# Hybrid decoder trunk on one core: order of the attention opening (dense keys and queries of head 0, value tiles, rotated queries of heads 2 and 3, key latents' sums)

## The chip, the cores and the metric

The kernel runs on one core of one Trainium2 chip. The metric is the device time of one execution in microseconds. Three runs of the kernel before gave 2683.34, 2685.63 and 2686.16 us; their median is 2685.63 us.

## What is computed

Two layers act on x of 1024 tokens by 1024 columns in float32. The part that matters here is one of the three mixers, the attention of each layer (MLA):

```
h = rms_norm(x);  p = h @ w_in                      # 1024 x 2640
c_q (384), c_kv (256), k_pe (64) = first 704 columns of p
q  = rms_norm(c_q) @ w_uq      # 4 heads x (128 plain + 64 rotary)
kv = rms_norm(c_kv) @ w_ukv    # 4 heads x (128 key + 128 value)
q_pe, k_pe -> rotated with cos and sin (k_pe is shared by the heads)
s = (q_nope @ k_nope^T + q_pe @ k_pe^T) / sqrt(192), causal
o = softmax(s) @ v             # then rms_norm over 512 columns
```

Beside it stand a gated linear attention and an RWKV-7 recurrence with a state per head. The three outputs go through w_out, and a gated feed-forward part with a convolution of width 3 ends the layer. A last rms_norm gives the output.

## The kernel before, in words

Everything is laid out with features on the 128 partitions and the 1024 tokens along the free dimension. A float32 product is made of three matmuls in the fast format: each operand is split into a rounded high part and a low rest, and `mm3` (line 97 issues every such matmul) sums high x high, high x low and low x high. A projection tile of 128 features over 8 blocks of 128 inputs is so 2 halves x 8 x 3 = 48 matmuls of 512 columns. The last five projection tiles of a layer (lines 738 to 753) are two of key latents (`ckv`) and three of query latents (`cq`). They alternate between two PSUM buffers ("big"), and each half is read from PSUM by ScalarE (line 744, high part), VectorE (line 745, low part) and ScalarE again (line 748 or 751, square). The squares are summed over the tiles into one buffer `acc` (tag T1, one buffer, so the query latents' `acc` takes the place of the key latents'). `stats` then sums `acc` over the partitions with eight one-column matmuls (line 731; the profile counts 16 records, as float32 goes in two passes) and makes the scale `rkv` (keys) or `rq` (queries) of each token.

Background work (generators in a list) is woven in by `spend`: each group of matmuls adds its nominal time, and for each 2.4 us of it (`Q_IN`; 0.9 in the attention) `tick` takes one step of every generator. `delay(n, gen)` lets n ticks go by first. At this place VectorE also runs a long elimination (lines 699 to 706) for the recurrence.

The opening of the attention (lines 1018 to 1100) then goes, in program order: load and split weights for the rotated queries of heads 0 and 1 (`wq_pe(0)`); load cos, sin and the key's rotary rows (`kraw`, and `krot` with its halves exchanged); `dense_w(0)`, the weights of head 0's plain keys and queries, through one staging buffer; `q_pe`, 18 matmuls for two heads' rotary queries, evacuated into `raw` (line 1055), four copies on ScalarE's queue that write `rot` with halves exchanged (line 1058), and `rope` (lines 1043 to 1045: POOL rot x sin, VectorE raw x cos, VectorE the sum); the split into `QP` (lines 1073, 1074) for heads 0 and 1; the key's rotation and its split `khh`, `kll` (lines 1076 to 1078); value tiles 0 to 3; a second `q_pe` for heads 2 and 3, split (lines 1085, 1086) and stored to `qdr` in DRAM by four stores on SyncE's queue (lines 1089, 1090), to be read back when head 2 comes; `Rk`, the token scales spread over the partitions (lines 1091 to 1095: transposes, ScalarE copies); value tiles 4 to 7; three ticks of the recurrence (`rwkv_chunks`, which takes its buffers from the weight pool, so it needs those of both `q_pe` back); and last `dense_k(0)` and `dense_q(0)`, 12 and 18 matmuls with their evacuations (lines 1111 to 1113 and 1123, 1124). A value tile is six matmuls into one of two PSUM banks "a" and a ScalarE copy (line 1039). `raw`, `rot` and the transposed attention weights `pT` (lines 1155, 1157) share the tag PT with two buffers.

Then for each head and block of queries: `scores` (line 97, softmax in lines 1137 to 1143), `trans` (line 1153: transposes of the weights, copied into `pT`), and `pv` (line 1164).

The order on each engine is fixed when the program is built. A planner takes the instructions in program order as priority, lets a later one go ahead where its own estimates say that an earlier one is not ready, and assigns buffers; at run time each engine goes through its list in order. So program order is a preference, and the trace shows for instance the second `q_pe` ahead of most value tiles. The second layer runs the same code.

Of the kernel before, what the change touches and what calls it, by code (L numbers as in the profile page):

```python
# [21 lines left out]
NT = T // 128  # L22
# [39 lines left out]
def trunk(ctx: ExitStack, tc: tile.TileContext, A, out, offs):  # L62
# [27 lines left out]
    def delay(n, gen):  # L90
        for _ in range(n):
            yield
        yield from gen
# [36 lines left out]
    def aps():  # L130
        return psp.tile([128, 512], F32, tag="a", name="psa")
# [172 lines left out]
    for l in range(DEPTH):  # L304
# [423 lines left out]
        def stats(acc, rs, width):  # L728
            sps = aps()
            for i in range(NT):  # L730
                pe.matmul(sps[:, i:i + 1], lhsT=acc[:, i * 128:(i + 1) * 128], rhs=ones, start=True, stop=True)
            act.activation(rs, sps[:, 0:NT], AF.Copy)
            rstd(rs, rs, NT, 1.0 / width, EPS)
            if rs is rq:
                pool.tensor_scalar(rq, rq, 192 ** -0.5, 1.0, ALU.mult, ALU.mult)
            yield

        for dst, K, gname, rs, width in ((ckv, 2, "mla_kv_norm_g", rkv, 256), (cq, 3, "mla_q_norm_g", rq, 384)):
            acc = tt(1, "acc")
            for k in range(K):  # L740
                ps = in_tile()
                g = col(gname, k)
                for n in range(2):
                    act.activation(dst[0][k][:, HALF[n]], ps[n], AF.Copy, scale=g)
                    dve.scalar_tensor_tensor(dst[1][k][:, HALF[n]], ps[n], g, dst[0][k][:, HALF[n]].bitcast(F32),
                                             ALU.mult, ALU.subtract)
                    if k == 0:
                        act.activation(acc[:, HALF[n]], ps[n], AF.Square)  # L748
                    else:
                        sq = rtp.tile([128, 512], F32, tag="csq", name="csq")  # L750
                        act.activation(sq, ps[n], AF.Square)
                        pool.tensor_tensor(acc[:, HALF[n]], acc[:, HALF[n]], sq, ALU.add)
            bg.append(delay(2, stats(acc, rs, width)))
        drain()
        tmps.close()
        right.close()
# [254 lines left out]
        def wq_pe(h):  # L1011
            return split_w(wp, 3, 128, [(64 * j, WQ[:, 192 * (h + j) + 128:192 * (h + j) + 192]) for j in range(2)])
# [4 lines left out]

        vwh, vwl = wq.pop(0)[0]
        w_pe = [wq_pe(0)]
        cos = pg("P", "cos", bufs=2)  # L1020
        sin = pg("P", "sin", bufs=2)
        nc.sync.dma_start(out=cos, in_=A["rope"][0])
        nc.sync.dma_start(out=sin, in_=A["rope"][1])
        kraw = pg("kn0", "kraw")
        krot = pg("kn1", "krot")
        for b in range(2):
            nc.sync.dma_start(out=kraw[64 * b:64 * b + 64, :], in_=kdr)
            nc.sync.dma_start(out=krot[64 * b:64 * b + 32, :], in_=kdr[32:64, :])
            nc.sync.dma_start(out=krot[64 * b + 32:64 * b + 64, :], in_=kdr[0:32, :])
        wts = dense_w(0, dve)  # L1030

        v = ap.tile([128, NT, 512], F32, name="v")

# [5 lines left out]
            act.activation(v[:, i, :], ps, AF.Copy, scale=rkv[:, i:i + 1])  # L1039
            spend(1.28)  # L1040

        def rope(raw, rot):
            pool.tensor_tensor(rot, rot, sin, ALU.mult)
            dve.tensor_tensor(raw, raw, cos, ALU.mult)
            dve.tensor_tensor(raw, raw, rot, ALU.add)

        def q_pe(w):
            ps = bigps()
            mtile(ps, 128, 3, w, cq)
            ps = halves(ps)  # L1050
            raw = pg("PT", "qraw", F32R, bufs=2)
            rot = pg("PT", "qrot", F32R, bufs=2)
            fr, ft = raw.bitcast(F32), rot.bitcast(F32)
            for n in range(2):
                act.activation(fr[:, HALF[n]], ps[n], AF.Copy)
            for b in range(4):
                o = 32 * (b ^ 1)
                nc.scalar.dma_start(out=ft[32 * b:32 * b + 32, :], in_=fr[o:o + 32, :])
            rope(fr, ft)
            return raw, rot  # L1060

        khh = pg("khh", "khh", F32R)
        kll = pg("kll", "kll", F32R)
        Rk = pg("Rk", "Rk")

        raw, _ = q_pe(w_pe.pop())
        w_pe.append(wq_pe(2))
        raw = raw.bitcast(F32)
        QP = []
        for j in range(2):  # L1070
            rows, orow = slice(64 * j, 64 * j + 64), slice(64 - 64 * j, 128 - 64 * j)
# [1 line left out]
            act.activation(q[rows, :], raw[rows, :], AF.Copy)  # L1073
            dve.tensor_tensor(q[orow, :], raw[rows, :], q[rows, :].bitcast(F32), ALU.subtract)
            QP.append(q)
        rope(kraw, krot)
        act.activation(khh, kraw, AF.Copy)
        dve.tensor_tensor(kll, kraw, khh.bitcast(F32), ALU.subtract)
        rb = pg("qn1", "rb")
        dve.tensor_copy(rb.rearrange("p (i d) -> p i d", i=NT),  # L1080
                        rkv.rearrange("p (i o) -> p i o", o=1).to_broadcast([128, NT, 128]))
        for i in range(4):
            v_tile(i)
        raw, rot = q_pe(w_pe.pop())
        act.activation(rot, raw.bitcast(F32), AF.Copy)
        dve.tensor_tensor(raw, raw.bitcast(F32), rot.bitcast(F32), ALU.subtract)
        for j in range(2):
            rows, orow = slice(64 * j, 64 * j + 64), slice(64 - 64 * j, 128 - 64 * j)
            nc.sync.dma_start(out=qdr[j][rows, :], in_=rot[rows, :].bitcast(F32))
            nc.sync.dma_start(out=qdr[j][orow, :], in_=raw[rows, :].bitcast(F32))  # L1090
        for b in range(2):
            ps = aps()
            for i in range(4):
                pe.transpose(ps[:, i * 128:(i + 1) * 128], rb[:, (4 * b + i) * 128:(4 * b + i + 1) * 128], ident)
            act.activation(Rk[:, b * 512:(b + 1) * 512], ps, AF.Copy)
        for i in range(4, 8):
            v_tile(i)
        bg.append(rwkv_chunks())
        for _ in range(3):
            tick()  # L1100

        heads = {}

# [120 lines left out]
                yield  # L1224

        heads[0] = (dense_k(0, wts[0]), dense_q(0, wts[1]), QP[0])
        t1 = t2 = None

        def flush(n):
# [9 lines left out]
        for h in range(4):  # L1239
            for at, i in enumerate((3, 4, 0, 5, 1, 6, 2, 7) if h == 0 else range(NT)):  # L1240
                if h == 3 and i == 0:
                    bg.append(early_wout())
                r = scores(h, i)
                if h < 3 and at == 3:
                    wts = dense_w(h + 1)
                if at == NT - 1 and h < 3:
                    kn = dense_k(h + 1, wts[0])
                    flush(1)
                    t1 = (h, i, *r)
                    qn = dense_q(h + 1, wts[1])  # L1250
                    if h == 0:
                        heads[1] = (kn, qn, QP[1])
                        Q2 = [None, None]
                        Q2[0] = pg("QP0", "QPr", F32R)
                        nc.sync.dma_start(out=Q2[0].bitcast(F32), in_=qdr[0])
                    elif h == 1:
                        heads[2] = (kn, qn, Q2[0])
                        Q2[1] = pg("QP1", "QPr", F32R)
                        nc.sync.dma_start(out=Q2[1].bitcast(F32), in_=qdr[1])
                    else:  # L1260
                        heads[3] = (kn, qn, Q2[1])
                else:
                    flush(1)
                    t1 = (h, i, *r)
# [521 lines left out]
```

## Time and profile before

| | |
|---|---|
| median of three runs | 2685.63 us |
| the profiled execution | 2680.95 us |
| its span | 2679.2 us |
| VectorE busy | 1686.9 us, 63% |
| ScalarE busy | 1154.1 us, 43% |
| POOL busy | 1049.1 us, 39% |
| mean granted TensorE clock | 0.983 of full |

The opening comes twice: in layer 0 the last projection matmul starts at 324.57 us and the first scores at 367.54 us. TensorE's busy time counts a matmul from start to its modelled end, so a stretch at half clock is busy too; the granted clock (PEclk) must be read beside it. In a timeline the bracket holds the idle time of the engine just before the instruction and what released it.

### The profile page before, as it was taken

The numbers are of one execution on the slowest core, as the hardware profiler recorded it, in microseconds if no ns is written. First come the engines' busy times: TensorE is split into PE (matmuls) and PEld (weight loads), VectorE is DVE, ScalarE is ACT, GpSimd is POOL, SyncE is SP. The second block draws the span as 40 slices with busy tenths as digits, with TensorE's granted clock in tenths as the row PEclk, the third lists the DMA queues.
The fourth block names the chain that finished last, engine by engine and source line by source line (L and its number), as shares of the span: only waits on it lengthen the run. The fifth ranks groups of instructions, "written<-read, shape, count | busy, mean of one in ns | idle before, by whom it ended". The sixth has DMA issues, their size and how long they took to land. (4 is left out here: it accounts for less than half of the span.)

```text
span 2679.2 us, 36147 instructions
## 1 busy us (share of the span) xinstructions
PE 2582.8 (96%) x13842; PEld 2093.7 (78%) x13842; DVE 1686.9 (63%) x2390; ACT 1154.1 (43%) x1894; POOL 1049.1 (39%) x903
## 2 busy tenths in 40 slices
PE   8999989999899999999999999999998999999997
PEld 7668778888778888777776787788886888887786
DVE  3446665655976666776733565656469756668775
ACT  4221255554544544543352222546444445455333
POOL 4446432132554444231234563323326544452311
PEclk9999999999999999999999999999999999999999
DMA  4102221133232222685411122212342222217941
GB/s 131 32 24 56 67 72 43 51 117 119 78 103 71 94 72 70 206 206 124 116 38 32 32 71 67 62 32 68 119 133 64 90 84 78 88 56 236 216 114 63
DMA packets 246333, 240.93 MB, mean 90 GB/s; under 512 B 40376, under 2 KB 188304, under 8 KB 246160
## 3 DMA queue, kind: packets, MB, share of 16 engines
q1 hardware_dynamic: 210816, 203.31, 24.1%
q0 software_dynamic: 14336, 27.27, 5.8%
q10 hardware_dynamic: 21008, 8.04, 1.2%
q8 instruction: 109, 1.79, 0.3%
q14 instruction: 64, 0.52, 0.1%
HBM read 178.80 MB, written 53.48 MB: 87 GB/s over the span
## 5 line engine op out<-in xcount | busy, mean ns | idle before, releaser
L97 PE MATMUL psb<-hl,wh 128*128 128x512 f32 (+2 forms) x704 | 269.8, 384 | 1.5 <-DVE hl L208 1.5
L97 PE MATMUL psb<-hh,wh 128*128 128x512 f32 (+2 forms) x704 | 266.4, 380 | 4.2 <-ACT acc L748 3.3
L97 PE MATMUL psb<-hh,wl 128*128 128x512 f32 (+2 forms) x704 | 268.7, 382 | 0.7 <-POOL wl L258 0.7
L97 PE MATMUL psr<-B,RG 128*128 128x512 f32 x1032 | 253.9, 391 | 0.7 <-DVE RG L1299 0.7
L97 PE MATMUL psa<-T,RG 128*128 128x512 f32 x1008 | 246.6, 390 | 1.0 <-ACT RG L1298 1.0
L1299 POOL TENSOR_TENSOR RG<-S_m,RG 128x512 fp32r<-128x512 f32 x86 | 121.5, 1412 | 274.2 <-ACT RG L1298 239.1
L97 PEld LDWEIGHTS psr<-B,RG 128*128 128x128 f32 x1032 | 193.5, 188 | 43.8 <-DVE RG L1299 1.6
L97 PEld LDWEIGHTS psa<-T,RG 128*128 128x128 f32 x1008 | 189.1, 188 | 42.5 <-ACT RG L1298 1.8
L1298 ACT ACTIVATE RG<-S_m 128x512 fp32r<-128x512 f32 x176 | 111.0, 630 | 226.3 <-PE psa L97 118.2
L97 PEld LDWEIGHTS psb<-hh,wl 128*128 128x128 f32 (+1 forms) x704 | 132.5, 188 | 33.4 <-issue 10.5
L97 PEld LDWEIGHTS psb<-hh,wh 128*128 128x128 f32 (+1 forms) x704 | 132.1, 188 | 33.5 <-issue 4.9
L97 PEld LDWEIGHTS psb<-hl,wh 128*128 128x128 f32 (+1 forms) x704 | 132.6, 188 | 29.5 <-issue 5.4
L97 PE MATMUL psr<-T,RG 128*128 128x512 f32 x528 | 136.4, 400 | 11.0 <-ACT T L1298 9.2
L97 PEld LDWEIGHTS psr<-T,RG 128*128 128x128 f32 x528 | 101.4, 192 | 35.5 <-ACT T L1298 10.1
L258 POOL TENSOR_TENSOR wl<-ws,wh 128x1024 fp32r<-128x1024 f32 (+1 forms) x40 | 91.4, 2287 | 92.3 <-ACT wh L256 61.4
L1496 DVE SCALAR_TENSOR_TENSOR psb<-uv,convc,psb 128x1023 f32<-128x1023 f32 x72 | 92.6, 1286 | 55.2 <-ACT psb L1494 54.2
L1298 ACT ACTIVATE de<-R 128x1024 fp32r<-128x1024 f32 x67 | 69.2, 1052 | 117.7 <-PE psb L97 35.5
L1606 POOL DMA_DIRECT2D R<-fdr x48 | 43.9, 945 | 187.6 <-issue 50.4
L97 PE MATMUL psb<-de 128*128 128x512 f32 x384 | 108.9, 402 | 6.6 <-DVE acc_kb L1677 6.6
L254 POOL TENSOR_TENSOR ws<-ws,pcol 128x1024 f32<-128x1024 f32 x36 | 76.5, 2127 | 87.2 <-DMA ws<-in_w_in 77.9
L256 ACT ACTIVATE wh<-ws 128x1024 fp32r<-128x1024 f32 (+2 forms) x44 | 43.7, 994 | 154.9 <-PE psb L97 146.1
L1299 DVE TENSOR_TENSOR de<-R,de 128x1024 fp32r<-128x1024 f32 x67 | 84.2, 1268 | 40.2 <-ACT de L1298 40.2
(552 smaller groups left out, 6590.5 us busy)
## 6 DMA issues: line engine op xcount, KB each, us to landing
wu_m<-in_ffn_w_up SPq DMA_DIRECT2D x88, 512.0 KB
fdr<-acc SPq DMA_DIRECT2D x44, 512.0 KB
R<-fdr SPq DMA_DIRECT2D x88, 256.0 KB
R<-in_ffn_w_down SPq DMA_DIRECT2D x88, 256.0 KB
ws<-in_w_in SPq DMA_DIRECT2D x38, 512.0 KB
R<-fdr POOLq DMA_DIRECT2D x48, 256.0 KB, 5.5
y_m<-ydr SPq DMA_DIRECT2D x16, 512.0 KB
xmid<-x SPq DMA_DIRECT2D x16, 512.0 KB
```

What stands on the lines that cost most here:

```text
L97: pe.matmul(o, lhsT=l, rhs=r, start=first, stop=last, skip_group_check=on)
L254: eng.tensor_tensor(ws, ws, g.rearrange("p (k o) -> p k o", o=1).to_broadcast([128, K, M]), ALU.mult)
L256: act.activation(wh, ws, AF.Copy)
L258: eng.tensor_tensor(wl, ws, wh.bitcast(F32), ALU.subtract)
L1298: act.activation(d[0], s, AF.Copy)
L1299: eng.tensor_tensor(d[1], s, d[0].bitcast(F32), ALU.subtract)
L1496: dve.scalar_tensor_tensor(a[:, d:T], u[:, 0:T - d], conv[:, 2 - d, jj:jj + 1], a[:, d:T], ALU.mult, ALU.add)
L1606: pool.dma_start(out=o, in_=x, accum_op=ALU.add)
```

## The change

Five things are moved, and nothing is computed differently.

1. `stats` of both latents waits six ticks in place of two.
2. The weights of head 0's dense keys and queries are loaded and split right behind `wq_pe(0)`, ahead of the loads of cos, sin and the key's rotary rows. `kraw` and `krot` take the buffers qn0 and qn1 (those of head 0's dense queries) in place of kn0 and kn1, and `rb`, from which `Rk` is made, takes kn1.
3. `rope` becomes `turn`, which makes the two products and leaves the sum to the caller. `Rk` is made right after the first `q_pe`, then come the key's two products, then the sum and split of the queries of heads 0 and 1, then the key's sum and split.
4. `dense_k(0)` and `dense_q(0)` come ahead of all value tiles; value tiles 0 to 3, the second `q_pe` (products only), value tiles 4 to 7 and the three ticks follow.
5. The sum and split of the queries of heads 2 and 3 and their four stores (`keep_q2`) come behind the first block's scores.

```diff
-            bg.append(delay(2, stats(acc, rs, width)))
+            bg.append(delay(6, stats(acc, rs, width)))
...
         w_pe = [wq_pe(0)]
+        wts = dense_w(0, dve)
         cos = pg("P", "cos", bufs=2)
...
-        kraw = pg("kn0", "kraw")
-        krot = pg("kn1", "krot")
+        kraw = pg("qn0", "kraw")
+        krot = pg("qn1", "krot")
...
-        wts = dense_w(0, dve)
...
-        def rope(raw, rot):
+        def turn(raw, rot):
             pool.tensor_tensor(rot, rot, sin, ALU.mult)
             dve.tensor_tensor(raw, raw, cos, ALU.mult)
-            dve.tensor_tensor(raw, raw, rot, ALU.add)
...
-            rope(fr, ft)
+            turn(fr, ft)
             return raw, rot
...
-        raw, _ = q_pe(w_pe.pop())
+        rb = pg("kn1", "rb")
+        dve.tensor_copy(rb.rearrange("p (i d) -> p i d", i=NT),
+                        rkv.rearrange("p (i o) -> p i o", o=1).to_broadcast([128, NT, 128]))
+        raw, rot = q_pe(w_pe.pop())
         w_pe.append(wq_pe(2))
+        for b in range(2):
+            ps = aps()
+            for i in range(4):
+                pe.transpose(ps[:, i * 128:(i + 1) * 128], rb[:, (4 * b + i) * 128:(4 * b + i + 1) * 128], ident)
+            act.activation(Rk[:, b * 512:(b + 1) * 512], ps, AF.Copy)
+        turn(kraw, krot)
         raw = raw.bitcast(F32)
+        dve.tensor_tensor(raw, raw, rot.bitcast(F32), ALU.add)
         QP = []
...
-        rope(kraw, krot)
+        dve.tensor_tensor(kraw, kraw, krot, ALU.add)
         act.activation(khh, kraw, AF.Copy)
         dve.tensor_tensor(kll, kraw, khh.bitcast(F32), ALU.subtract)
-        rb = pg("qn1", "rb")
...
-        for i in range(4):
-            v_tile(i)
-        raw, rot = q_pe(w_pe.pop())
-        act.activation(rot, raw.bitcast(F32), AF.Copy)
-        dve.tensor_tensor(raw, raw.bitcast(F32), rot.bitcast(F32), ALU.subtract)
...
         heads[0] = (dense_k(0, wts[0]), dense_q(0, wts[1]), QP[0])
+        for i in range(4):
+            v_tile(i)
+        raw2, rot2 = q_pe(w_pe.pop())
+        for i in range(4, 8):
+            v_tile(i)
+        bg.append(rwkv_chunks())
+        for _ in range(3):
+            tick()
+
+        def keep_q2():
+            dve.tensor_tensor(raw2.bitcast(F32), raw2.bitcast(F32), rot2.bitcast(F32), ALU.add)
+            act.activation(rot2, raw2.bitcast(F32), AF.Copy)
+            dve.tensor_tensor(raw2, raw2.bitcast(F32), rot2.bitcast(F32), ALU.subtract)
+            for j in range(2):
+                rows, orow = slice(64 * j, 64 * j + 64), slice(64 - 64 * j, 128 - 64 * j)
+                nc.sync.dma_start(out=qdr[j][rows, :], in_=rot2[rows, :].bitcast(F32))
+                nc.sync.dma_start(out=qdr[j][orow, :], in_=raw2[rows, :].bitcast(F32))
...
                 r = scores(h, i)
+                if h == 0 and at == 0:
+                    keep_q2()
```

## Rows read from the trace of the kernel before

**Rows 1.** The page, part 1: busy us, share of the span, instructions, by engine.
```profile
PE 2582.8 (96%) x13842; PEld 2093.7 (78%) x13842; DVE 1686.9 (63%) x2390; ACT 1154.1 (43%) x1894; POOL 1049.1 (39%) x903
```

**Rows 2.** Waits of TensorE, whole span: who waited for whom, us in total, times, longest.
```profile
PE psa L731 <- POOL acc L752: 5.8, 4, 2.5
PE psb L97 <- DVE kn L1113: 5.2, 2, 3.9
...
PE psr L840 <- DMA rcb<-zdr: 3.5, 2, 2.5
PE psb L97 <- ACT acc L748: 3.3, 1, 3.3
```

**Rows 3.** Timeline, ScalarE, layer 0: start us, us, instruction, [idle before, releaser].
```profile
282.96 1.06 ACT L256 ACTIVATE wh<-ws 128x1024 fp32r<-128x1024 f32 x1 [0.81 <-PE psb L97]
...
295.54 0.60 ACT L751 ACTIVATE csq<-psb 128x512 f32<-128x512 f32 x1 [1.93 <-DVE ckv_m L745]
...
301.82 1.06 ACT L256 ACTIVATE wh<-ws 128x1024 fp32r<-128x1024 f32 x1 [2.17 <-PE psb L97]
...
313.89 1.06 ACT L321 ACTIVATE vwh<-vws 128x1024 fp32r<-128x1024 f32 x1 [6.97 <-PE psb L97]
...
324.77 0.52 ACT L256 ACTIVATE wh<-ws 128x384 fp32r<-128x384 f32 x1 [5.15 <-PE psb L97]
```

**Rows 4.** Timeline, TensorE, layer 1, sums of the key latents.
```profile
1625.79 1.05 PE L731 MATMUL psa<-ones,acc 128*128 128x1 f32 x8 [0.43 <-POOL acc L752]
...
1629.20 1.86 PE L731 MATMUL psa<-ones,acc 128*128 128x1 f32 x8 [1.55 <-POOL acc L752]
```

**Rows 5.** Timeline, ScalarE, layer 1, the same stretch as rows 3.
```profile
1627.12 0.60 ACT L751 ACTIVATE csq<-psb 128x512 f32<-128x512 f32 x1 [2.17 <-DVE ckv_m L745]
...
1633.02 1.06 ACT L256 ACTIVATE wh<-ws 128x1024 fp32r<-128x1024 f32 x1 [1.74 <-PE psb L97]
...
1645.05 1.06 ACT L321 ACTIVATE vwh<-vws 128x1024 fp32r<-128x1024 f32 x1 [6.92 <-PE psb L97]
```

**Rows 6.** Windows: busy us (instructions) of PE, PEld, DVE, ACT, POOL; PEclk, DMA share, GB/s.
```profile
324.60:367.50 42.90, 37.12 (x276) 28.90 (x274) 24.92 (x26) 22.10 (x39) 21.60 (x20) 0.98 0.41 100
1655.80:1699.00 43.20, 38.57 (x276) 29.95 (x274) 23.70 (x26) 22.32 (x39) 21.59 (x20) 0.96 0.41 99
367.50:377.50 10.00, 9.61 (x56) 7.61 (x56) 6.90 (x17) 4.28 (x9) 3.34 (x4) 0.59 0.46 128
```

**Rows 7.** Timeline, TensorE: sums of the query latents; first scores of each layer.
```profile
331.76 0.95 PE L731 MATMUL psa<-ones,acc 128*128 128x1 f32 x8
...
367.54 1.62 PE L97 MATMUL psb<-kn,qn 128*128 128x512 f32 x3 [3.93 <-DVE kn L1113]
...
1699.05 1.00 PE L97 MATMUL psb<-kn,qn 128*128 128x512 f32 x3 [1.31 <-DVE kn L1113]
```

**Rows 8.** Timeline, VectorE, end of the key rotation; queries of heads 2, 3 (layer 1).
```profile
357.46 1.22 DVE L1078 TENSOR_TENSOR kll<-kraw,khh 128x1024 fp32r<-128x1024 f32 x1
...
1693.05 1.23 DVE L1044 TENSOR_TENSOR qraw<-qraw,cos 128x1024 f32<-128x1024 f32 x1 [1.50 <-DMA qrot<-qraw]
...
1696.56 1.74 DVE L1045 TENSOR_TENSOR qraw<-qraw,qrot 128x1024 f32<-128x1024 f32 x1 [0.83 <-POOL qrot L1043]
1698.22 0.68 DVE L1113 TENSOR_TENSOR kn<-psb,kn 128x512 fp32r<-128x512 f32 x1
```

**Rows 9.** Timeline, layer 1, ScalarE's and SyncE's queues: copies, stores, first transposed weights.
```profile
1688.35 1.89 ACTq L1058 DMA_DIRECT2D qrot<-qraw  x3
...
1702.54 1.11 SPq L1090 DMA_DIRECT2D qdr<-qraw  x2
...
1706.61 0.60 ACT L1155 ACTIVATE pT<-psa 128x512 f32<-128x512 f32 x1 [0.75 <-PE psa L1153]
```

**Rows 10.** Timeline, layer 0, POOL and VectorE side by side.
```profile
348.37 2.56 POOL L1043 TENSOR_TENSOR krot<-krot,sin 128x1024 f32<-128x1024 f32 x1
...
348.61 3.40 DVE L1045 TENSOR_TENSOR qraw<-qraw,qrot 128x1024 f32<-128x1024 f32 x1
```

More of the change, by code (lines that the diff above doesn't have):

```diff
@@ L1075, in trunk @@
             QP.append(q)
-        rope(kraw, krot)
+        dve.tensor_tensor(kraw, kraw, krot, ALU.add)
         act.activation(khh, kraw, AF.Copy)
         dve.tensor_tensor(kll, kraw, khh.bitcast(F32), ALU.subtract)
-        rb = pg("qn1", "rb")
-        dve.tensor_copy(rb.rearrange("p (i d) -> p i d", i=NT),
-                        rkv.rearrange("p (i o) -> p i o", o=1).to_broadcast([128, NT, 128]))
-        for i in range(4):
-            v_tile(i)
-        raw, rot = q_pe(w_pe.pop())
-        act.activation(rot, raw.bitcast(F32), AF.Copy)
-        dve.tensor_tensor(raw, raw.bitcast(F32), rot.bitcast(F32), ALU.subtract)
[L1087 to L1100, printed above, removed]
         heads = {}
```

## The prediction

> **What bounds the kernel now.** I read the engines' shares first: TensorE is busy for 96% of the span [rows 1], so a change pays only where TensorE waits, or where its clock is at half because it waited. The list of its waits comes next [rows 2], and both places of this change stand in it: the sums of the key latents wait 5.8 us for POOL (four waits, two in each layer), and the first scores wait 5.2 us for the low part of head 0's keys (once in each layer). Then the timelines, to see what ends each wait, and the windows, for the clock. Behind the wait of 3.93 us at 367.54 [rows 7] the granted clock of ten microseconds is 0.59, that is mostly 1.2 GHz in place of 2.4 [rows 6]: a loss of 10 x 0.41 = 4.1 us that no wait row shows. That is my price for one fall of the clock.
>
> **Part 1: the sums, four ticks later.** ScalarE's weight splits mark the ends of projection tiles, as each waits for the tile that held its buffer. From 313.89 to 324.77 an undisturbed tile takes 10.88 us [rows 3]; 282.96 to 301.82, the first query tile, takes 18.86, and the next 12.07. So 7.98 + 1.19 = 9.2 us lie above the full-speed length in layer 0. Waits are 5.8 - 0.43 - 1.55 = 3.8 of it [rows 2, 4], the rest is the sums themselves and the half clock behind them.
>
> Four ticks are 4 x 2.4 us of nominal time, at 0.64 a group 15 groups or 45 matmuls, at 10.88 / 48 = 0.227 us each about 10 us. The sums fall into the second query tile, and `acc`, complete when the sums now run (1629.20 in layer 1 [rows 4]), is then no longer awaited. But not all of 9.2 us comes back, because the next thing is late: the second query tile needs the PSUM buffer of the last key tile, which is free only when ScalarE's second square ends, at 295.54 + 0.60 = 296.14 [rows 3]. This square waits for VectorE's reading, which stands in VectorE's list between steps of the elimination and does not depend on when TensorE does its sums. The first query tile would end at 282.96 + 10.88 = 293.84, so TensorE waits 2.3 us there. Then 10.88 for the tile and 0.95 for sums at full clock [rows 7] give 307.97 against 313.89: 5.9 us earlier. Whether the clock holds through 2.3 us of idleness is not shown; it costs 0 to 4.1, and I take 1, as dense matmuls stand on both sides of it. Gain in layer 0: 4.9.
>
> In layer 1 the first query tile ends at 1633.02 [rows 5]. Taking out the two waits (1.98), the sums (1.05 + 1.86, [rows 4]) and some 1 us of half clock behind them puts its end at 1627.1; the bank is free at 1627.12 + 0.60 = 1627.72. Adding 11.83 gives 1639.55 against 1645.05: 5.5 earlier. Together part 1 is worth 10.4 us. Its ends: 14, if no bank wait counts, and a loss (below, third rival). The delay for the query latents' sums adds nothing: no tile follows them, and the remaining generators are drained at once.
>
> **Part 2: what comes before the first scores.** From the last projection matmul to the first scores are 42.9 and 43.2 us, with 37.1 and 38.6 of TensorE work in them [rows 6], some of the latter at half clock. None of that work is added or removed; only its order changes. The wait that goes is that for the keys' low part: 3.93 and 1.31 [rows 7], with the clock's 4.1 behind the first. Why it waits is seen in layer 1 [rows 8]: VectorE goes through its list in order, and ahead of the keys' low part at 1698.22 stand the product and the sum of the queries of heads 2 and 3 (1693.05 and 1696.56), which no one needs before head 2 and which waited 1.50 for copies and 0.83 for POOL. With dense keys and queries first in program order, the eight value tiles and the second `q_pe` are what TensorE does while these are evacuated. Gain: 3.93 + 4.1 + 1.31 = 9.3.
>
> What is late next. The dense queries are written over `kraw` and `krot`, so their evacuation waits for the key's split, which ends at 357.46 + 1.22 = 358.68, 34.1 us behind the last projection [rows 8]. An evacuation of one half adds about 1.4 (ScalarE 0.6 and VectorE 0.68 for the like keys [rows 8, 9]), so the first scores can start at 35.5, while TensorE has work until 37.1, and until 39.0 with the waits that I leave in place. Cover: 3.5 us. If it is gone, each microsecond costs one, and then a fall of the clock. The wait for the recurrence's block (3.5 in both layers, [rows 2]) I leave as it is: its load needs a buffer that the second `q_pe` gives back, and that comes later now. The two weight loads moved ahead on SyncE's queue are no cost: before, the loads behind which they stood were not awaited by TensorE either. `rb` and `Rk` use the same instructions earlier, beside matmuls.
>
> `keep_q2` is the cost. Its sum, copy, difference and four stores hold both PT buffers, and `pT` of the first block needs one. In layer 1 the sum starts at 1696.56 and the last stores are issued by 1703.65 [rows 8, 9]: 7.1 us. A landing takes some 2.8 (copies issued by 1690.24, awaited until 1693.05, [rows 8, 9]). Put behind the scores (1.2 us of matmuls, estimated from [rows 7]), the buffers come free 11.1 us after the first scores start. `pT` was first written 1706.61 - 1699.05 = 7.6 us after them [rows 7, 9]. So ScalarE may wait 3.5 us in each layer. TensorE has the scores of other blocks and the recurrence meanwhile, so it loses between 0 and 3.5 + 4.1; I take 1 each, near the lower end, since two PSUM buffers of scores are free then. Part 2: 9.3 - 2 = 7.3.
>
> A rule bears on the order of the sums on VectorE. In [rows 10] VectorE's sum takes 3.40 us beside POOL's product, which ends at 350.93, against 1.22 for a like subtraction alone [rows 8]; 350.93 - 348.61 = 2.32 is the difference. The Trainium skill, SBUF — State Buffer, Who interferes with whom, says that a VectorE instruction with two SBUF inputs and a POOL instruction that reads SBUF exclude each other, and the one that comes second waits for the whole of the first. By that rule, which this row bears out, `keep_q2`'s sum and difference can each lose up to a POOL instruction's length in front of the softmax: with 2.3 us for each of four, the sum would be 9 us smaller. By the rows alone the softmax's own matmul cover hides most of it, and I keep the sum above.
>
> **Sum.** 10.4 + 7.3 = 17.7 us off the profiled execution's 2680.95, so 2663.3. That execution is 4.7 below the median of the runs shown, 2685.63; on the median's scale the forecast is 2668.
>
> **Rivals.**
>
> *Only the sums pay.* The opening's wait moves to the PT buffers: 3.5 + 4.1 in place of 3.93 + 4.1 in layer 0, 3.5 in place of 1.31 in layer 1. For it: the ring has two buffers and both are held. Against it: TensorE has other work. Time: 2685.6 - 10.4 + 1.8 = 2677.
>
> *Everything goes.* The recurrence's load wait (3.5) goes too, with the bank wait hidden (14 in place of 10.4) and `pT` free of cost: 2685.6 - 14 - 9.3 - 3.5 = 2659. For it: planned order is new everywhere. Against it: the bank is freed by VectorE, which the change does not relieve.
>
> *The sums' gain is eaten by their own buffer.* The first query tile's squares write the same `acc`, so they must wait for the later sums, and with them its PSUM bank, which the third query tile needs. By my times the sums end near 304 and the bank at 306, against 308: 2 us to spare. If it fails, the nearest row is the 3.3 us wait for such a square [rows 2], with a fall of the clock 7.4 in each layer: 2685.6 - 17.7 + 14.8 = 2683, no change that can be measured.
>
> *Slower: the key's rotation becomes the bound.* Place: the dense queries' evacuation at the head of ScalarE's list, waiting for `kraw`'s buffer, with the value tiles' copies behind it; TensorE, with two banks for these, stops. With a slip of x us in the rotation, TensorE waits x - 3.5 in each layer and the clock falls in both: 2(x - 3.5) + 8.2 against the 9.3 + 10.4 gained, so it decides from x = 9 on. At x = 12: 5.5 us slower, 2691. For it: ScalarE, POOL and VectorE are in order, and the queries' copies are late already (1.50 in [rows 8]). Against it: 9 us is a lot in a chain of 34.
>
> **Chances.** Forecast 0.50, own range 2662 to 2675; only the sums 0.22; everything 0.08; buffer eats the gain 0.12; slower 0.08. A difference under 0.2% (5.4 us) can't be told from no change in measurements of this kernel. Faster than 2680.3: 0.50 + 0.08 + nine tenths of 0.22 = 0.78. Within 0.2%: the rest of 0.22 and 0.12, 0.14. Slower: 0.08. The range goes from 2656, a little under the case in which everything goes, to 2687, which leaves out the slower case alone.
>
> **What would show it.** The waits of the key latents' sums for POOL are gone; instead one matmul of the second query tile waits for a square, some 2.3 us in layer 0 and under 1 in layer 1. The first scores come 38 to 40 us after the last projection matmul, with no wait for the keys and PEclk at 1.0 in the ten microseconds behind. `pT`'s first copy waits for stores, not for transposes. I am wrong if the sums still wait, if the stretch from projection to first scores keeps its 43 us, or if a new wait over 3 us with half clock behind it stands in the first blocks of scores.

## The result and the profile after

The changed kernel takes 2703.14 us (median of four runs, 2698.72 to 2705.99) against 2685.89 for the kernel before on the same chip: ratio 1.0057, interval 1.0040 to 1.0073. It is 15 us slower by the ratio, where 17.7 us faster was forecast. A second set of runs of the same kernel gave 1.0052 (1.0040 to 1.0065).

The profiled execution took 2705.99 us. I read its page's first part (busy us, share, instructions), then TensorE's waits over the whole span (us in total, times, longest), which answer to [rows 1, 2].

```profile
PE 2601.5 (96%) x13842; PEld 2104.6 (78%) x13842; DVE 1699.3 (63%) x2390; ACT 1153.5 (43%) x1894; POOL 1039.5 (38%) x903
```
```profile
...
PE psa L97 <- ACT v L1039: 5.2, 1, 5.2
PE psb L97 <- DVE de_m L1305: 5.0, 2, 3.5
PE psb L97 <- ACT acc L748: 4.9, 2, 4.2
PE psb L97 <- ACT wh L1003: 4.2, 4, 1.8
...
```

TensorE executes the same 13842 instructions and is busy 18.7 us longer (2601.5 against 2582.8). More than half of that is a lower clock: the mean granted clock is 0.979 against 0.983, which makes some 11 us (an estimate, 2704.2 x 0.021 less 2679.2 x 0.017). The two waits that the change was to remove are gone from this list, the key latents' sums' for POOL and the first scores' for the keys. New are one wait for a value tile's copy (5.2 us), some waits for weights of the small tiles (line 1003), and one of 3.5 us at line 1305, far from the change, which the last section takes up. In layer 1 the first scores still wait, now 1.28 us for the low part of head 0's queries (line 1111) where it was 1.31 for the keys. But these waits do not add up to the loss. It shows in the windows (busy us and instructions of PE, PEld, DVE, ACT, POOL, then PEclk, DMA share, GB/s), first from the last projection matmul to the first scores in both layers, then ten microseconds of the first blocks of scores; they answer to [rows 6].

```profile
323.70:369.20 45.50, 37.96 (x161) 28.95 (x161) 20.97 (x21) 18.81 (x34) 20.29 (x19) 0.85 0.34 79
1674.40:1712.70 38.30, 33.25 (x168) 26.00 (x168) 22.61 (x21) 17.51 (x31) 18.79 (x19) 0.91 0.41 100
...
379.20:389.20 10.00, 10.00 (x55) 8.10 (x54) 5.62 (x16) 4.10 (x9) 0.00 (x0) 0.50 0.43 108
```

The whole stretch from the end of the last projection matmul to the output projection grew from 244.2 to 257.1 us in layer 0 and from 240.9 to 250.5 in layer 1: 22.5 of the 25.0 us by which these two profiled spans differ (2704.2 and 2679.2). Its granted clock fell from 0.98 to 0.95 and from 0.99 to 0.97. What ends it is seen on TensorE's timeline. First the opening of layer 0 (start us, us, instruction, [idle before, releaser]), to be read against [rows 7]:

```profile
358.31 0.80 PE L97 MATMUL psa<-vwh,ckv_m 128*128 128x512 f32 x1 [5.17 <-ACT v L1039]
...
369.21 0.84 PE L97 MATMUL psb<-kn,qn 128*128 128x512 f32 x3
...
372.16 0.69 PE L840 MATMUL psr<-rcb,SC 32*32 32x32 f32 x16
```

The last row is step 3 of the recurrence's first block; in the kernel before it started at 345.45, so it is 26.7 us later, while the first scores are only 1.7 us later than in [rows 7]. Then the end of the attention, the kernel before and then the changed kernel. L1164 and L1151 are the last products with the values, L911 the end of the recurrence's step 7.

```profile
565.08 2.00 PE L1164 MATMUL psa<-v,pT 128*128 128x128 f32 x16
566.92 0.61 PE L911 MATMUL psr<-St,rcb 128*128 128x128 f32 x4
```
```profile
572.67 1.28 PE L1151 MATMUL psa<-v,pT 128*128 128x128 f32 x10
...
576.74 1.08 PE L907 MATMUL psr<-rcb,SC 128*128 128x64 f32 x8 [1.14 <-DVE rcb L898]
...
579.01 0.71 PE L911 MATMUL psr<-St,rcb 128*128 128x128 f32 x4
...
580.88 1.43 PE L97 MATMUL psr<-wo_m,yhl_m 128*128 128x512 f32 x5 [0.71 <-ACT rcb L916]
```

Before, attention and recurrence end together, within 2 us. After, the attention is done and the recurrence goes on alone, 6.3 us in layer 0 and, in the rows below, 14.5 us in layer 1, where the granted clock is 0.71 over the stretch.

```profile
1907.24 0.71 PE L1151 MATMUL psa<-v,pT 128*128 128x128 f32 x4
...
1921.71 1.17 PE L911 MATMUL psr<-St,rcb 128*128 128x128 f32 x4
```
```profile
1907.00:1922.00 15.00, 13.83 (x111) 11.82 (x106) 6.05 (x20) 3.81 (x10) 2.64 (x5) 0.71 0.26 84
```

### The profile page after: what moved, and what is told of

Its sections match the earlier page's. It is cut to its first block, busy times and chain, and to the rows that moved or that the text cites. A ratio compares the mean times of both kernels' runs of the same rounds, so it can differ in the third digit from the quotient of the medians.

```text
span 2704.2 us, 36173 instructions
## 1 busy us (share of the span) xinstructions
PE 2601.5 (96%) x13842; PEld 2104.6 (78%) x13842; DVE 1699.3 (63%) x2390; ACT 1153.5 (43%) x1894; POOL 1039.5 (38%) x903
## 5 line engine op out<-in xcount | busy, mean ns | idle before, releaser
L1502 DVE SCALAR_TENSOR_TENSOR psb<-ug,convc,psb 128x1023 f32<-128x1023 f32 x72 | 92.4, 1283 | 24.9 <-ACT psb L1500 23.9
```

The source lines that it names most:

```text
L1502: dve.scalar_tensor_tensor(a[:, d:T], u[:, 0:T - d], conv[:, 2 - d, jj:jj + 1], a[:, d:T], ALU.mult, ALU.add)
```

## The experiments

Theory A: the second `q_pe`, now behind the dense tiles and half the value tiles, gives its weight buffers back some 28 us later in layer 0 (its first matmul at 363.60 in place of 335.4); the recurrence takes its own buffers from there, so it starts late, and as a chain of steps that can't be shortened it ends the attention. Theory B: the later sums cost. Theory C: the value tiles' copies stuck on ScalarE's list (the 5.17 us above) and the half clock behind them cost. The table gives each run's median, its ratio to the kernel before run beside it (whose median was 2685.9 to 2687.8 from round to round, so the ratios are what to compare), and three times of layer 0 from its profile: step 3 of the first recurrence block, the last value product, and line 911 of the last step 7.

| kernel | us | ratio (interval) | step 3 | value | step 7 |
|---|---|---|---|---|---|
| before | 2685.9 | | 345.5 | 565.1 | 566.9 |
| changed | 2703.1 | 1.0057 (1.0040 to 1.0073) | 372.2 | 572.7 | 579.0 |
| changed, again | 2701.4 | 1.0052 (1.0040 to 1.0065) | 373.2 | 572.7 | 579.1 |
| sums only | 2683.1 | 0.9986 (0.9975 to 0.9998) | 344.7 | 565.1 | 567.0 |
| opening only | 2705.4 | 1.0068 (1.0049 to 1.0087) | 368.8 | 559.6 | 575.5 |
| second q early | 2681.0 | 0.9979 (0.9968 to 0.9989) | 348.7 | 562.6 | 566.6 |
| second q late | 2711.3 | 1.0094 (1.0075 to 1.0112) | 369.6 | 574.9 | 578.9 |
| faster ticks | 2701.1 | 1.0049 (1.0035 to 1.0063) | 373.1 | 572.9 | 580.0 |
| own weights | 2690.7 | 1.0014 (1.0004 to 1.0025) | 335.5 | 567.2 | 571.2 |
| recurrence first | 2681.2 | 0.9977 (0.9965 to 0.9990) | 348.2 | 564.0 | 565.9 |
| recurrence mid | 2680.4 | 0.9972 (0.9959 to 0.9985) | 347.8 | 565.0 | 566.8 |
| own weights, early | 2687.0 | 1.0002 (0.9993 to 1.0011) | 335.7 | 576.5 | 565.3 |
| load on SyncE | 2682.4 | 0.9975 (0.9963 to 0.9987) | 349.3 | 564.7 | 566.6 |
| scaling on VectorE | 2701.7 | 1.0050 (1.0038 to 1.0063) | | | |

**Sums only.** The kernel before with

```
-            bg.append(delay(2, stats(acc, rs, width)))
+            bg.append(delay(6, stats(acc, rs, width)))
```

> Only the later start of the latents' column sums (six turns of the background work instead of two), the opening of the attention as before. Theory A (the loss is the later second query-position tile, which starts the recurrence late; the later sums pay): TensorE no longer waits for GpSimd's sum of squares in the projection, about 2 us in layer 0 and 5 us in layer 1, so 2677 to 2682 us. Theory B (the later sums themselves cost, by waits for ScalarE's square and the lower clock that follows): 2686 us or more.

It is faster by 0.5 to 6.7 us, 3.8 by the ratio: theory B falls. The median, 2683.05, lies just above the 2682 that I expected. The profile shows what took the sums' place in layer 0, TensorE's wait for ScalarE's square. The second row, of layer 1, is no new wait; the third is its like in the kernel before.

```profile
297.80 0.50 PE L97 MATMUL psb<-hh,wh 128*128 128x512 f32 x1 [2.10 <-ACT csq L751]
```
```profile
1616.71 0.80 PE L97 MATMUL psb<-hh,wh 128*128 128x512 f32 x1 [3.99 <-ACT acc L748]
```
```profile
1614.41 0.50 PE L97 MATMUL psb<-hh,wh 128*128 128x512 f32 x1 [3.34 <-ACT acc L748]
```

The first is the bank wait of the prediction (2.3 us). Behind it the granted clock from 297 to 304 is 0.76, against 0.52 in the kernel before.

**Opening only.** The changed kernel with the first edit undone:

```
-            bg.append(delay(6, stats(acc, rs, width)))
+            bg.append(delay(2, stats(acc, rs, width)))
```

> Only the new opening of the attention, the column sums after two turns as before. Theory A: the whole loss and more sits here, 2705 to 2712 us, with the recurrence's steps some 16 us later than in the kernel before in layer 0 and the recurrence alone on TensorE at the attention's end. Theory B: about as the kernel before, 2680 to 2690 us.

Theory A's range holds, and the whole loss is here. In layer 0's opening no matmul waits over 0.4 us for a value tile's copy in this run, so theory C falls too: the loss is as large without it. The copies into `pT` that wait for `keep_q2`'s stores are a further rival; they wait less here (1.33 and 1.21 us in layer 0, 0.97 in layer 1) than in the changed kernel (4.68 and 0.46, 2.22 and 1.55), and the loss is no smaller. The rows of the recurrence's start, the last value product and the end show the two chains apart, and windows show what it costs to run alone.

```profile
368.84 0.69 PE L840 MATMUL psr<-rcb,SC 32*32 32x32 f32 x16
```
```profile
559.60 0.71 PE L1151 MATMUL psa<-v,pT 128*128 128x128 f32 x4
...
571.21 1.94 PE L907 MATMUL psr<-rcb,SC 128*128 128x64 f32 x8 [0.30 <-DVE rcb L898]
...
575.50 1.17 PE L911 MATMUL psr<-St,rcb 128*128 128x128 f32 x4
```
```profile
540.00:560.00 20.00, 20.00 (x207) 18.03 (x206) 11.11 (x27) 10.73 (x24) 4.96 (x8) 1.00 0.21 67
560.00:575.00 15.00, 13.83 (x95) 11.72 (x95) 5.68 (x19) 3.31 (x10) 1.53 (x3) 0.63 0.26 84
575.00:580.00 5.00, 4.69 (x15) 3.58 (x15) 1.63 (x5) 1.66 (x5) 3.48 (x6) 0.50 0.24 53
```

The attention alone is 5.5 us earlier than before (559.60 against 565.08): the new opening does for the scores what the prediction said. But the recurrence ends 8.6 us later, and from 560 on the clock is 0.63, then 0.50: eight matmuls of line 907 take 1.94 us there and 1.08 at full clock.

**Second q early.** The changed kernel with the tile's matmuls moved, its split left behind the first scores:

```
+        raw2, rot2 = q_pe(w_pe.pop())
         heads[0] = (dense_k(0, wts[0]), dense_q(0, wts[1]), QP[0])
         for i in range(4):
             v_tile(i)
-        raw2, rot2 = q_pe(w_pe.pop())
```

> The changed kernel with the second query-position tile moved back ahead of the dense keys and queries (its split stays behind the first scores); it so gives its weight buffers back before the value tiles, though the recurrence is still started behind them. Theory A (late weight buffers hold the recurrence): the first recurrence block's step 3 comes some 15 to 20 us earlier than in the changed kernel, the last recurrence step again ends with the last attention product, and the time is 2680 to 2690 us. Rival C (the loss is the value tiles' copies behind the key's rotation on ScalarE, and the lower clock after it): the five-microsecond wait at the value tiles stays, and the time with it, 2697 to 2705 us.

By this one move the kernel goes from 1.0057 to 0.9979: 0.78%, 21 us. Step 3 comes 23.5 us earlier. The ends in layer 0:

```profile
562.60 1.95 PE L1151 MATMUL psa<-v,pT 128*128 128x128 f32 x16
564.38 1.00 PE L907 MATMUL psr<-rcb,SC 128*128 128x64 f32 x8
...
566.58 0.71 PE L911 MATMUL psr<-St,rcb 128*128 128x128 f32 x4
```

They stand 4 us apart. The wait for the value tiles' copy went too, and so did those of `pT` for the stores, so against these two rivals this run alone would say nothing; the run above does.

**Second q late.** The kernel before, the tile moved the other way, the recurrence's start with it (its buffers are not there earlier):

```
-        raw, rot = q_pe(w_pe.pop())
...
-        bg.append(rwkv_chunks())
...
         heads[0] = (dense_k(0, wts[0]), dense_q(0, wts[1]), QP[0])
+        raw, rot = q_pe(w_pe.pop())
...
+        bg.append(rwkv_chunks())
```

> The kernel before with one thing moved: the second query-position tile, its split and the recurrence's start stand behind the dense keys and queries of head 0 instead of between the value tiles. Key rotation, value tiles and dense tiles are in the old order. Theory A: the recurrence's step 3 of its first block comes at about 370 us instead of 345, its last step ends alone, and the time rises by 10 to 20 us, 2696 to 2706 us. Rival C (value tiles behind the rotation): nothing of that changes here, 2680 to 2688 us.

It costs 25 us, more than expected, with step 3 at 369.6 as said. Here the recurrence does not end alone; the attention is as late (574.9 against 578.9). The windows show why: TensorE lacks its filler at the start.

```profile
340.00:355.00 15.00, 9.16 (x33) 6.41 (x32) 10.15 (x7) 5.15 (x8) 5.89 (x2) 0.77 0.42 97
...
370.00:385.00 15.00, 11.93 (x125) 10.05 (x123) 11.13 (x20) 4.86 (x11) 2.96 (x2) 0.75 0.36 75
385.00:400.00 15.00, 14.81 (x119) 12.79 (x117) 6.39 (x22) 6.88 (x17) 1.75 (x3) 0.80 0.18 45
```

In the kernel before the first of these has 13.97 us of TensorE work at a clock of 1.00, and the last 1.00. From 400 to 560 TensorE is busy over 98% in both, so nothing lost ahead of 400 is won back. The expectation that the last step ends alone was wrong for this kernel.

**Faster ticks.** The changed kernel with

```
-Q_IN, Q_ATT, Q_OUT, ELIM = 2.4, 0.9, 1.6, 5
+Q_IN, Q_ATT, Q_OUT, ELIM = 2.4, 0.7, 1.6, 5
```

> The changed kernel with a tick of background work in the attention for each 0.7 us of nominal matmul time instead of 0.9. If the late start is what costs and the recurrence is by then a chain of dependent steps that can't go faster (207 us from step 3 of the first block to the last step 7 in layer 0 of the changed kernel, 221.5 in the kernel before), the length stays at 203 to 207 us and the time at 2698 to 2706 us. If it is only its place in the order, the faster ticks win the delay back: 190 to 200 us of length, the last step 7 beside the last attention product, 2685 to 2693 us.

From step 3 (373.08) to line 911 of the last step 7 (580.03) are 206.95 us, and 205.64 in layer 1. The same length is 206.85 and 204.51 in the changed kernel, 205.86 and 204.21 in its second profile, 206.66 and 204.52 in the one with the opening only, 209.26 and 207.60 with the second tile late; in kernels that start it early it is 213 to 238, as then TensorE, full of attention, sets the pace. So some 205 us is the shortest that the recurrence takes in this planned order, and the ticks don't shorten it. With the last value product at 565 in the kernel before, step 3 must start by about 565 - 206 = 359 us; at 372 it ends the attention.

**Own weights.** The changed kernel, in its order; only the tile's weights come from another ring:

```
-        w_pe.append(wq_pe(2))
...
         heads[0] = (dense_k(0, wts[0]), dense_q(0, wts[1]), QP[0])
+        w2 = w_small(3, 128, [(64 * j, WQ[...heads 2, 3...]) for j in range(2)], dve)
...
-        raw2, rot2 = q_pe(w_pe.pop())
+        raw2, rot2 = q_pe(w2)
```

> The changed kernel, order and all, but the weights of the second query-position tile are loaded into the ring of the dense tiles' weights instead of the weight pool, so the recurrence's buffers no longer wait for that tile. Theory A as to buffers: step 3 of the first block comes at 345 to 355 us although the second query-position tile is as late as in the changed kernel, and the time is 2678 to 2688 us. If the place of the tile in the order matters by itself (its matmuls, its copies on ScalarE's queue, the temporaries it holds), step 3 stays behind 365 us or the time stays above 2695 us.

```profile
335.48 1.03 PE L840 MATMUL psr<-rcb,SC 32*32 32x32 f32 x16 [2.20 <-DMA rcb<-zdr]
```
```profile
325.00:400.00 75.00, 67.09 (x464) 54.31 (x466) 42.94 (x76) 35.46 (x70) 21.32 (x19) 0.89 0.33 78
```

The tile is as late as in the changed kernel, and step 3 starts 36.7 us earlier than there: the buffers are what held the recurrence. But 2690.66 lies between my two ranges. Of the 0.78% between the changed kernel and the one with the tile early, 0.43% comes back with the buffers. The rest may hang on the tile's place. Over 325 to 400 the clock is 0.89 here, 0.93 before and 0.98 with the tile early, and the same stretch of layer 1 has 0.89, 0.98 and 0.95: without the tile's 18 matmuls TensorE has less to do while the keys are turned. The rows fit that; no run shows it alone. In layer 0 a value tile's copy (2.47 us) and `pT` (1.38 and 1.65, for the stores) are waited for here too, and neither with the tile early, so what makes up the rest stays open.

**Recurrence first, recurrence mid.** As "second q early", with the recurrence put on the list earlier. The first has the added line ahead of value tile 0, the second here:

```
         for i in range(4):
             v_tile(i)
+        bg.append(rwkv_chunks())
         for i in range(4, 8):
             v_tile(i)
-        bg.append(rwkv_chunks())
```

> The second query-position tile ahead of the dense tiles, as in the run before that did this, and the recurrence also put on the list of background work ahead of the value tiles instead of behind them. If the start of the recurrence still sets the attention's end (there its last step 7 came 4 us behind the last attention product in both layers), step 3 of the first block comes earlier than 345 us, the two end together and the time is 2670 to 2677 us. If the recurrence no longer ends last, the time stays at 2680 to 2684 us.

> As the run with the recurrence put on the list ahead of the value tiles, but between value tiles 3 and 4. By the start-time theory it lies between that run and the one with the start behind the value tiles: 2672 to 2680 us. If the start no longer matters: 2680 to 2684 us.

Both are faster than before and neither differs measurably from "second q early". But step 3 came no earlier (348.2 and 347.8 against 348.7, 24.5 to 24.6 us behind the projection in all three), as it waits 3.4 us for its load. So neither run tests what an earlier start is worth. In layer 0 the two chains end within 2 us of each other; in layer 1 of "recurrence mid" they are still 4 us apart (1892.04 and 1896.02). "Recurrence mid" has the lowest median of all that ran, 0.28% under the kernel before (0.15 to 0.41).

**Own weights, early.** As "recurrence mid", but the tile right behind the dense tiles, with weights of its own:

```
-        w_pe.append(wq_pe(2))
...
-        raw2, rot2 = q_pe(w_pe.pop())
         heads[0] = (dense_k(0, wts[0]), dense_q(0, wts[1]), QP[0])
+        w2 = w_small(3, 128, [(64 * j, WQ[...heads 2, 3...]) for j in range(2)], dve)
+        raw2, rot2 = q_pe(w2)
```

> The second query-position tile's weights in the dense weights' ring, the tile itself right behind the dense tiles and ahead of the value tiles, the recurrence put on the list between value tiles 3 and 4. If it was the late tile itself (its matmuls beside no other wait) that kept the run with own weights at 2691 us, this comes to 2672 to 2680 us, with no wait for the recurrence's step 3. If the ring's third load (staging, split on VectorE) costs the rest, 2684 to 2692 us.

This gained nothing. 2686.97 lies in the second range, but its reason, the ring's third load, is not shown by these rows; they show the other chain ending last:

```profile
565.29 0.61 PE L911 MATMUL psr<-St,rcb 128*128 128x128 f32 x4
...
576.49 1.95 PE L1150 MATMUL psa<-v,pT 128*128 128x128 f32 x16
```

Now the recurrence is done 11 us ahead of the attention's last value product. It may have taken TensorE from the scores, as the mirror of the changed kernel, and the first scores themselves come 49.2 us behind the projection, 46.0 in "recurrence mid"; how the 0.30% against "recurrence mid" comes about, I did not settle.

**Load on SyncE.** "Recurrence mid" with the first block's load on another queue:

```
         def load_z(p):
-            nc.scalar.dma_start(...)
+            (nc.scalar if p else nc.sync).dma_start(...)
```

> The run with the recurrence put on the list between value tiles 3 and 4, but with the first recurrence block's small load issued on SyncE's queue instead of ScalarE's, where it stood behind the four copies that exchange halves. If its place in ScalarE's queue is why TensorE waited 3.4 us for it in each layer, that wait goes, with the half clock behind it: 2672 to 2677 us. If the load lands late because the key's and query's copies fill the DMA queues anyway, the wait stays and the time is 2678 to 2683 us.

The wait fell from 3.40 to 1.66 us (and from 3.48 to 0.96 in layer 1), but the time is no other (0.9975 against 0.9972), and step 3 came no earlier. The issue of the load, first in "recurrence mid", then on SyncE's queue:

```profile
342.01 0.34 ACTq L784 DMA_DIRECT2D rcb<-zdr  x1
```
```profile
344.27 0.65 SPq L784 DMA_DIRECT2D rcb<-zdr  x1
```

Counted from the end of the projection the load was issued 1.5 us later here, not earlier (20.3 us behind it against 18.8), and step 3 started 0.7 us later (25.3 against 24.6); in layer 1 it was 4.6 and 1.4 us later. TensorE had only less idle time in front of it. So the run does not show whether the place in ScalarE's queue held the load.

**Changed, again; scaling on VectorE.** The first is the changed kernel as it is; the second moves the scaling (line 254) of two weight tiles:

```
+        first = [l > 0]
...
         def next_w():
-            prefetch()
+            prefetch(dve if first.pop() else None)
+            first.append(False)
             return wq.pop(0)
...
         wq.pop(0)
         wq.pop(0)
-        prefetch()
+        prefetch(dve if l else None)
```

> The changed kernel as it is, for a second profiled execution: in the first, TensorE stood still for 3.5 us at the end of layer 0's down-projection and ran at half clock behind it, where GpSimd and VectorE held each other up, and about 7.5 us went there. If which of the two comes first changes from one execution to the next, the second profile may lack that stop and be about 7 us shorter; if the schedule fixes it, the stop is there again, and the time is 2699 to 2706 us as before.

> The changed kernel with the scaling of the first two weight tiles that layer 1 loads during its projection done by VectorE instead of GpSimd. If the stop of 3.5 us at the end of layer 0's down-projection came from GpSimd and VectorE holding each other up, it is gone and the profiled execution is 4 to 8 us shorter than the first of the changed kernel. If VectorE is simply late there, its two added operations of 1.2 us make the stop longer, and the time is 2703 us or more.

These are about the stop at line 1305. Its rows follow in the last section. The stop is there in the first profile of the changed kernel and not in the second, whose span is 6.4 us shorter (2697.8), so the order of the program does not fix it. With the scaling moved it is not there either, the profiled span 4.2 us under the first of the changed kernel; as the unmoved kernel can lack it too, this one profile does not show that the move removes it. The median is the same as the changed kernel's (1.0050 against 1.0052).

## Why the prediction was wrong

The step that failed is the sentence on the recurrence: "The wait for the recurrence's block (3.5 in both layers, [rows 2]) I leave as it is: its load needs a buffer that the second `q_pe` gives back, and that comes later now." I saw the link and priced it at nothing, by looking at the wait it had caused so far and not at the chain behind it. What the runs showed in its place: step 3 starts 26.7 us later in layer 0, and the recurrence then ends the attention, 6.3 us (layer 0) and 14.5 us (layer 1) after the last value product starts. Moving the tile back is worth 0.78%, 21 us (second q early). The buffers alone are worth 0.43%, some 11.5 us (own weights); the cause of the rest is open. None of the rivals named it; the slower one had another place.

The other steps, in order:

- *The sums, mechanism.* Right. The key latents' waits for POOL are gone, and the second query tile waits for ScalarE's square, 2.10 us in layer 0 and 0.57 in layer 1, where 2.3 and under 1 were forecast. A new wait of 0.92 us for POOL stands in layer 0 at the query latents' sums, whose delay was to add nothing.
- *The sums, size 10.4.* Too large; alone they are worth 3.8 us by the ratio (0.5 to 6.7). ScalarE's weight splits, as in [rows 3, 5], in the second profile of the changed kernel:

```profile
284.89 1.05 ACT L256 ACTIVATE wh<-ws 128x1024 fp32r<-128x1024 f32 x1
...
312.72 1.06 ACT L321 ACTIVATE vwh<-vws 128x1024 fp32r<-128x1024 f32 x1 [1.32 <-PE psb L97]
```

  From the one to the other are 27.83 us, against 313.89 - 282.96 = 30.93: 3.1 us gained, not 4.9; the same two rows of layer 1 give 26.31 against 30.79, 4.5 gained, not 5.5. In layer 0 the start of this stretch is itself 1.9 us later (0.8 in the first profile). Two terms were mis-sized. I took 0.95 us for the sums, the length of one row of [rows 7], but that row is eight of the sixteen records; all sixteen take 1.84 (second profile):

```profile
306.87 1.84 PE L731 MATMUL psa<-ones,acc 128*128 128x1 f32 x16
```

  And the half clock behind the bank wait, which I took at 1 us, is 7 x (1 - 0.76) = 1.7.
- *The first scores 38 to 40 us behind the projection, with no wait for keys.* No wait for keys is left, but one for the low part of the queries is, 1.28 us in layer 1 (and 1.52 in layer 0 of "opening only"):

```profile
1712.71 0.96 PE L97 MATMUL psb<-kn,qn 128*128 128x512 f32 x3 [1.28 <-DVE qn L1111]
```

  So there the wait changed its place rather than went. In layer 1 the first scores come after 38.3 us; in layer 0 after 45.5, though with the opening alone after 38.5. The 7 us of layer 0 go with the wait of 5.17 and the low clock around it (0.85 over the stretch), and are the slower rival in small. ScalarE's split of the queries waits 5.00 for VectorE's sum at line 1077, with the value tiles' copies behind it. That sum runs 2.81 us from 350.99, and POOL's product of the key ends at 349.35 + 3.38 = 352.73; 1.07 us remain, an undisturbed sum's length, 1.21 at line 1085, nearly. It agrees with the rule of the Trainium skill cited in the prediction, SBUF — State Buffer, Who interferes with whom; I had applied it to `keep_q2` alone.
- *`pT`'s first copy waits for stores.* Right: it waited 4.68 us in layer 0 and 2.22 in layer 1 for the stores to `qdr`, where 3.5 was forecast. What TensorE lost by it stands in no row by itself: the clock of 0.50 from 379 to 389 falls together with the recurrence's late start.
- *Part 2, size 7.3.* It shows as the 5.5 us by which the last value product of "opening only" is earlier, and is not paid out. Even with the tile early, the kernel is only 2 us from "sums only" (2680.95 and 2683.05), which can't be told from none.

So two terms had the right sign and were far smaller than forecast, and the move whose price was set at nothing cost more than the forecast of both together.

## What to carry to other kernels

When an operation is moved back, follow the buffers it gives back as closely as the results it makes, down to the end of the chain that takes them; a long chain that runs beside a full engine has a latest start, here about 206 us ahead of the attention's end, and a slip past it counted nearly in full: 13 us past it in layer 0 of the changed kernel, an end 12 us later. The wait that the chain showed so far says nothing of that price: 1.0 and 2.5 us at this place before, and 21 us for moving it. Cheap filler matmuls that stand in a stretch of dependences keep TensorE busy and its clock up, and moving them out is not free: in "second q late" 9.16 us of work and a clock of 0.77 are left of 13.97 and 1.00, from 340 to 355.

## What the runs showed of the hardware

VectorE and POOL held each other up whole instructions at a time, and which of them lost was decided by a fraction of a microsecond (POOL 0.42 us ahead of VectorE's line 1638, or 0.11 us behind its line 1305). At the end of layer 0's down-projection, the first profile of the changed kernel has these rows of POOL, VectorE and TensorE:

```profile
1313.46 1.89 POOL L254 TENSOR_TENSOR ws<-ws,pcol 128x1024 f32<-128x1024 f32 x1 [4.85 <-DVE de_va L1305]
1315.74 1.91 POOL L254 TENSOR_TENSOR ws<-ws,pcol 128x1024 f32<-128x1024 f32 x1 [0.39 <-DMA ws<-in_w_in]
```
```profile
1313.88 2.02 DVE L1638 SCALAR_TENSOR_TENSOR R<-R 128x512 f32<-128x512 f32 x1
1315.83 2.91 DVE L1305 TENSOR_TENSOR de_m<-R,de_m 128x1024 fp32r<-128x1024 f32 x1
```
```profile
1318.79 0.75 PE L97 MATMUL psb<-de_m,de_m 128*128 128x512 f32 x2 [3.47 <-DVE de_m L1305]
```

The second profile of the same kernel has, at the same place:

```profile
1311.44 6.95 POOL L254 TENSOR_TENSOR ws<-ws,pcol 128x1024 f32<-128x1024 f32 x1 [4.92 <-DVE R L1638]
...
1318.35 1.89 POOL L254 TENSOR_TENSOR ws<-ws,pcol 128x1024 f32<-128x1024 f32 x1
```
```profile
1310.73 0.69 DVE L1638 SCALAR_TENSOR_TENSOR R<-R 128x512 f32<-128x512 f32 x1
1311.33 1.22 DVE L1305 TENSOR_TENSOR de_m<-R,de_m 128x1024 fp32r<-128x1024 f32 x1
...
1315.41 1.22 DVE L1305 TENSOR_TENSOR de_va<-R,de_m 128x1024 fp32r<-128x1024 f32 x1
...
1318.43 2.89 DVE L1305 TENSOR_TENSOR de_m<-R,de_sg 128x1024 fp32r<-128x1024 f32 x1 [0.68 <-ACT de_sg L1304]
```

Where POOL is first, its operations take 1.9 us each, VectorE's take 2.02 and 2.91 in place of 0.69 and 1.22, and TensorE stops for 3.47 us and goes on at half clock. Where VectorE is first, its times are the short ones, and TensorE has no wait over 0.5 us. POOL's first operation then takes 6.95 us: six VectorE operations that read two tiles in SBUF go by in a row, and it ends 1.8 us behind the last of them (the one at 1315.41). Its second, ahead again, takes 1.89, and VectorE's line 1305 beside it 2.89. Ahead of this place the second profile is 2.1 us earlier (POOL's last issue at line 1612, 1305.66 against 1307.75), behind it 6.1 us (the end of VectorE's line 1305 from `de_sg`, 1321.32 against 1327.41): 4.0 us lie in who came first. The stop of 3.4 to 3.5 us was in three of the profiled executions (the changed kernel, "recurrence first", "load on SyncE"), and in none of the others. The rule of the Trainium skill above says that the one that issues first holds the shared ports for its whole instruction, and these rows agree.

The spans of two profiles of the same kernel differ so by 6.4 us, 4.0 of it at a place far from the change; with one profile alone these would have been put down to the change.
